# Mixing begun at the first half of the first value chunk, and the value pairs' weight sums formed on GpSimd

## The chip, the cores and the metric

The kernel runs on one core of one Trainium2 chip. A core has a matrix engine (TensorE, PE in the profile, whose weight loads are shown apart as PEld), three engines for elementwise work (VectorE or DVE, ScalarE or ACT, GpSimd or POOL) and SyncE (SP), which here only issues the transfers of weights. Each engine takes its instructions in the order in which they stand in its own queue and waits for the others through semaphores. The metric is the time of one execution in microseconds (us).

## The reference, cut to what matters

A trunk of two layers over 256 tokens and a model width of 2048, all in 32-bit floats. The change lies in the second layer, which is an mLSTM with 8 heads:

```python
hn = rmsnorm(h, o_norm[j])
u = hn @ o_w_in[j]                       # q|k (2048), v (2048), og (2048), z (2048), 16 gates
qk = jax.nn.silu(causal_conv(qk, c_conv_w[j], c_conv_b[j]))      # 4 taps
q, k = qk[..., :C_QK], qk[..., C_QK:]    # 8 heads of 128 each
li = ig + c_b_i[j]
lf = jax.nn.log_sigmoid(fg + c_b_f[j])
yc = mlstm(q, k, v.reshape(bsz, s, 8, 256), li, lf)
yc = head_rmsnorm(yc, c_norm[j]) * jax.nn.sigmoid(og) * jax.nn.silu(z)
h = h + yc @ o_w_out[j]
...
# mlstm, for every head:
wts = jnp.exp(dmat - m_t[..., None])              # decay weights from the gates
sc  = jnp.einsum('bhtd,bhsd->bhts', qc, kc) * wts # scores
num = ... + jnp.einsum('bhts,bhse->bhte', sc, vc) # scores times values
den = ... + jnp.sum(sc, axis=-1)
hout = num / jnp.maximum(jnp.abs(den), jnp.exp(-m_t))[..., None]
```

## The kernel before, in words

**Products.** A 32-bit product is made of three matmuls in the fast format of PE: each operand is split into a high part (`hi`) and a remainder (`lo`), and hi·hi, hi·lo and lo·hi are added. Weights come as tiles of 128x1024 (512 KB). SP loads a tile into a ring `raw` of five buffers; ACT casts it to `whi` (L137, or L221 in `split_weights`), DVE subtracts to get `wlo` (L138, or L222), and PE runs 12 matmuls of 512 columns on it for each half of the tokens. `whi` and `wlo` have four buffers each, so DVE has to write one `wlo` of 128x1024 for each tile that PE uses.

**Pairs of chunks.** The columns of a weight matrix are done in pairs of chunks of 512 (`seven`, L288 to L382). For one quarter of the contraction seven products take the place of eight (Strassen's scheme); they need *sums of weight tiles*. The tiles X and Y lie in buffers `ch`. One sum is formed by an accumulating transfer that GpSimd issues (`add_loaded`, L314), others by a two-operand addition of 128x1024 (`add`, L310): X+Y after product 5, and X+Z when products 2 and 6 are both done. The rest of the contraction (letters a and b) is done plainly with tiles from the ring. The string `a5a6.2aA7b.4F.bb` gives the order of the steps; a point, and every plain piece, lets the other work in hand (`lanes`) go one step on. At "A" the first half of the tokens of the first chunk is handed out, at "F" the second half.

**The value stage.** `value_halves` runs two such pairs over the value columns: pair 0 gives the chunks j = 0 and 1, pair 1 the chunks 2 and 3. `values` turns each half (hf = 0, 1) of a chunk into a high part `vt` (ACT, L1394) and a remainder `vl` (DVE, L1395).

**Mixing.** `mix(j)` handles the heads 2j and 2j+1: PE spreads the running maximum over the partitions (`spread`, L431, out of a tile `s` that DVE makes at L426), DVE forms `wt` (L1305, L1306), ACT takes its exponential (L1310, L1311); ACT and DVE split q and k into `qhl` and `khl` (L1322, L1323); PE forms the scores (L1329, and L1330 for a block that needs one matmul only); DVE multiplies them by `wt` (L1331); ACT casts them to `sh` (L1334), DVE makes `sl` (L1335); then PE multiplies scores by values into `nu` (L1349), for mix(0) with the values of chunk 0. The values of q and k come from `features`: for each, ACT's L1214 and L1215, six instructions of DVE (L1218, the taps) a pair of heads, tanh on ACT (L1221) and a last product on DVE (L1222). Before that the q and k columns take a way through memory, by transfers that GpSimd issues (L686, L689). `gate_stats` (L1257 to L1285) makes the maximum from the gate columns, in small instructions of DVE.

In the kernel before, the four mixes are started when the *second* half of chunk 0 has been handed out ("F" of pair 0). The program is written in that order, and a scheduler puts each instruction into its engine's queue by priorities that follow the order of the program, with splits, additions and mix's splits moved forward (`tc.high_priority`). So the place at which a lane is started decides where its matmuls stand among PE's products, and everything on the engines is in order behind it.

Of the kernel before, what the change touches and what calls it, by code (L numbers as in the profile page):

```python
# [16 lines left out]
ALU = mybir.AluOpType  # L17
# [28 lines left out]
def trunk(ctx: ExitStack, tc: tile.TileContext, a, out):  # L46
    nc = tc.nc
    v, s, gp, te, sy = nc.vector, nc.scalar, nc.gpsimd, nc.tensor, nc.sync
# [28 lines left out]
    def pump():  # L77
        with ExitStack() as behind:
            for ins in last.values():
                behind.enter_context(tc.issue_after(ins))  # L80
            for lane in list(lanes):
                step(lane)
# [40 lines left out]
    def block(src, c, n):  # L123
        return src[c * P:(c + n) * P].rearrange("(p n) -> p n", p=P)
# [92 lines left out]
    def split_weights(r):  # L217

        hi, lo = (wp.tile([P, 1024], F32R, name=n, tag=n) for n in ("whi", "wlo"))
        with tc.high_priority(offset=400):  # L220
            last["act"] = s.copy(hi, r).ins  # L221
            last["dve"] = v.tensor_tensor(out=lo, in0=r, in1=hi.bitcast(F32), op=ALU.subtract).ins  # L222
        return hi, lo
# [14 lines left out]
    def stationary(act, js, hf):  # L238
        return [[tokens(act[j][x], k, hf) for j in js for k in range(2)] for x in range(2)]

    def plain(w, j, kq, act, ps, first=(False, False), end=False):

        parts = load_weights(w[4 * j + kq])
        for hf in range(2):
            product(ps[hf], stationary(act, (2 * kq, 2 * kq + 1), hf), parts, first[hf], end)
            if hf == 0:
                pump()
# [37 lines left out]
        keep(d, (2, 4))  # L285
        yield

    def seven(w, j, act, qs, kqs, room, part, home=None, order=None, acc=None, before=None, third=None):  # L288

        def src(b, side, kq):  # L290
            return block(w[4 * (j + b) + kq], side * 1024, 1024)

        def load(tile_of, b, side):
            tiles = []
            for kq in kqs:
                t = tile_of()
                last["sp"] = sy.dma_start(out=t, in_=src(b, side, kq)).ins
                tiles.append(t)
            return tiles

        def ring():
            return wp.tile([P, 1024], F32, name="raw", tag="raw", bufs=5)

        def split(tiles):
            return [split_weights(t) for t in tiles]

        def add(x, y):
            with tc.high_priority(offset=400):
                for xi, yi in zip(x, y):
                    v.tensor_tensor(out=xi, in0=xi, in1=yi, op=ALU.add)  # L310

        def add_loaded(x):
            for xi, kq in zip(x, kqs):
                gp.dma_start(out=xi, in_=src(1, 0, kq), accum_op=ALU.add)  # L314

        def soon(out, in0, in1, op):
            with tc.high_priority(offset=450):
                v.tensor_tensor(out=out, in0=in0, in1=in1, op=op)

        def keep(out, bank):  # L320
            with tc.high_priority(offset=450):
                s.copy(out, bank)

        def quadrant(side, hf):
            return stationary(act, [2 * kq + side for kq in kqs], hf)

        def combo(n):
            return [[t for kq in kqs for t in qs[n, kq][x]] for x in range(2)]

        if acc is None:  # L330
            acc = len(kqs) == 2
        rest = [kq for kq in range(4) if kq not in kqs]
        E = px.tile([P, 512], F32, name="mx", tag="mx")
        A, F, B = (pm.tile([P, 512], F32, name="mm", tag="mm") for _ in range(3))
        b5, g = part(), part()
        rows = [list(rest), list(rest)]
        X = load(room, 0, 0)
        product(A, quadrant(0, 0), split(X), True)
        if acc:
            add_loaded(X)  # L340
        with tc.high_priority(offset=450):
            if home is not None:
                with tc.issue_after(last["act"]):
                    s.copy(E, home)
            s.copy(F, A)
            s.activation(B, F, AF.Copy, scale=-1.0)
        if third is not None:
            plain(w, j + 2, kqs[0], act, third, (True, True))
        Y = load(room, 1, 1)
        product(E, combo(4), split(Y), home is None)  # L350
        W = X
        if not acc:
            W = load(ring, 1, 0)
            add(Y, W)
            add(W, X)
        did = set()
        for op in order or ORDERS[len(kqs)]:
            if op in "ab":
                b = "ab".index(op)
                kq = rows[b].pop(0)  # L360
                if before is not None:
                    before(kq)
                plain(w, j + b, kq, act, ((A, F), (E, B))[b], end=not rows[b])
            elif op == "5":
                product(B, combo(1), split(W))
                add(X, Y)
                if acc:
                    add_loaded(Y)
                keep(b5, B)
            elif op == "6":  # L370
                product(B, combo(2), split(X))
                keep(g, B)
            elif op == "2":
                Z = load(ring, 0, 1)
                product(A, quadrant(1, 0), split(Z))
            elif op == "4":
                product(F, quadrant(1, 1), split(X))
            elif op == "7":
                product(B, combo(3), split(Y))
                soon(b5, B, b5, ALU.subtract)  # L380
            elif op == ".":
                pump()  # L382
            elif op == "A":
                yield 0, 0, A
            elif op == "F":
                soon(b5, F, b5, ALU.subtract)
                yield 0, 1, b5
            did.add(op)
            if op in "26" and {"2", "6"} <= did:
                add(X, Z)  # L390
        if home is None:
            soon(g, E, g, ALU.add)
            yield 1, 0, g
        else:
            soon(home, E, g, ALU.add)
            yield 1, 0, None
        yield 1, 1, B
# [243 lines left out]
    acth = []  # L641
# [133 lines left out]
    if True:  # L775
        ew = a["ew"]
        fs, qs, ks, xcs = {}, {}, {}, {}
# [281 lines left out]
        vts = []  # L1059
# [74 lines left out]
    act = out_proj(hq, mixed(), "fe")  # L1134
# [23 lines left out]
    acth = ple_gate(hq, two_and_seven(a["g0"], act, ready(act, "fe"), (e0, "q4", 2), in_e0), pls, rp0, hss0, "on", "fg", gate_sums)  # L1158
# [34 lines left out]
    with tc.tile_pool(name="m1", bufs=2) as m1:  # L1193
# [32 lines left out]
        qs = {}  # L1226
# [17 lines left out]
        vts = []  # L1244
# [132 lines left out]
        def value_halves():  # L1377
            drain("combos")
            pr = pieces(m1.tile([P, 1024], F32, name="pr", tag="vt", bufs=6))
            yield from seven(a["ov"], 0, acth, qs, (0,), chain, pr, acc=True)  # L1380
            drain("spill")
            store_of.extend(hp.tile([P, 1024], F32, name="pr", tag="h") for _ in range(2))
            for b, hf, src in seven(a["ov"], 2, acth, qs, (0,), chain, part, acc=True):
                yield 2 + b, hf, src

        def values():
            for j, hf, src in value_halves():
                if hf == 0:
                    vt = m1.tile([P, 2, 2, VW], F32R, name="vt", tag="vt", bufs=6)
                    gp.memset(vt.bitcast(F32)[:, :, :, 256:VW], 1.0)  # L1390
                    vl = ap.tile([P, 1024], F32R, name="vl", tag="ahl").rearrange("p (h i e) -> p h i e", h=2, i=2)
                with tc.high_priority(offset=450):
                    src = src.rearrange("p (i e) -> p i e", i=2)
                    s.activation(vt[:, hf, :, 0:256], src, AF.Copy, scale=norm["rt"][:, hf:hf + 1])  # L1394
                    v.scalar_tensor_tensor(vl[:, hf], src, norm["rt"][:, hf:hf + 1], vt[:, hf, :, 0:256].bitcast(F32),  # L1395
                                           op0=ALU.mult, op1=ALU.subtract)
                if hf == 0:
                    continue
                vts.append((vt, vl))
                if j == 0:  # L1400
                    drain("qk0", "qk2")
                    for c in range(4):
                        start("mix", mix(c))
                    start("mix", mix_norm())
# [4 lines left out]
        def part():  # L1409
            n = len(turn) % 4  # L1410
            turn.append(n)
            return store_of[n // 2][:, n % 2 * 512:(n % 2 + 1) * 512]
# [28 lines left out]
        for jj in (0, 2):  # L1441
            us = [m1.tile([P, 2, 512], F32, name="u", tag="vt", bufs=6) for _ in range(2)]
            for b, hf, src in pair(a["oz"], jj, True):
                j, u = jj + b, us[b]
# [59 lines left out]
        act, qs1 = {}, {}  # L1504
# [232 lines left out]
```

## Time and profile before

| | us |
|---|---|
| median of 3 runs | 1028.01 |
| lowest, highest | 1027.76, 1029.28 |
| the profiled execution | 1028.51 |
| its span | 1026.7 |

The profiled execution took 0.5 us more than the median, and 1.8 us of it lie outside of the span. The mean granted clock of PE was 0.994 of full speed. Times inside the trace are counted from the span's start. The value stage is the stretch from 561 us (first product of pair 0) to 649 us; pair 1 begins at about 605 us.

How such rows are read: in the page's list of engines, each engine has its busy time, its share of the span and its count of instructions. A row of the list of waits says which instruction waited for which, with the total, the times and the longest. A row of the timeline is: start, duration, engine, line, operation, output <- inputs, size, and in brackets the idle time just before it with what ended it. Durations of a row overlap with the next by the pipeline's depth, so the time that an instruction takes of its engine is read from start to start.

### The profile page before, as it was taken

The page shows a single profiled execution, that of the slowest core. Times are in us where ns is not written, and L with a number is a line of the kernel's source. Part 1 is how long each engine was busy: PE and PEld are TensorE (multiplying, and loading weights), DVE is VectorE, ACT ScalarE, POOL GpSimd, SP SyncE. Part 2 cuts the span into 40 slices and gives each one's busy share as a digit, 9 for nine tenths or more (in the row PEclk, how much of TensorE's full clock was granted, in tenths as well). Part 3 has the DMA queues.
Part 4 walks back from the last instruction along what each step waited for, and adds up shares of the span by engine and source line. Part 5 has one row for each costly group of instructions (what it writes and reads, how often), then busy time and mean ns, then how long its engine had stood idle before and what let it go on. Part 6 is the DMA issues. An engine that isn't in the chain of part 4 may idle for free.

```text
span 1026.7 us, 14530 instructions
## 1 busy us (share of the span) xinstructions
PE 1011.9 (99%) x5152; PEld 838.6 (82%) x5152; DVE 850.5 (83%) x1242; ACT 665.8 (65%) x956; POOL 103.5 (10%) x184
## 2 busy tenths in 40 slices
PE   9999999999999999999999999899999999999996
PEld 8888888888888888878888877688888888888886
DVE  7858968969686888879579998778989997899794
ACT  7775554686974555567557877676666867465562
POOL 0111101011111111022021100000011110111000
PEclk9999999999999999999999999899999999999998
DMA  9987756567688799588897856447879889686852
GB/s 360 335 223 250 222 175 203 167 200 238 221 263 303 246 298 286 165 263 254 290 314 217 263 166 219 163 155 204 251 194 296 237 236 354 198 284 210 283 184 83
DMA packets 69960, 243.18 MB, mean 237 GB/s; under 512 B 9056, under 2 KB 10464, under 8 KB 69888
## 3 DMA queue, kind: packets, MB, share of 16 engines
q1 hardware_dynamic: 55872, 197.56, 57.5%
q0 software_dynamic: 13584, 44.18, 16.4%
q8 instruction: 40, 0.66, 0.3%
q10 hardware_dynamic: 432, 0.52, 0.1%
q14 instruction: 32, 0.26, 0.1%
HBM read 222.31 MB, written 19.92 MB: 236 GB/s over the span
## 4 chain that ended last, share of the span: by engine, by line
PE 89%; DVE 7%; issue 1%; ACT 1%; DMA 1%; ACTq 0%; DVEq 0%; POOLq 0%
PE mm L235 27%; PE mm L211 12%; PE mm L213 12%; PE mm L212 12%; PE mx L235 8%; PE mx L213 3%; PE mx L212 3%; PE mx L211 3%; DVE wlo L138 2%; DVE qk L1218 2%; DVE wlo L222 1%; PE mm L517 1%; PE nu L1349 1%; PE mx L517 1%; PE mm L1562 1%
## 5 line engine op out<-in xcount | busy, mean ns | idle before, releaser
L138 DVE TENSOR_TENSOR wlo<-raw,whi 128x1024 fp32r<-128x1024 f32 (+1 forms) x305 | 366.1, 1211 | 101.8 <-ACT whi L137 96.2
L137 ACT CAST whi<-raw 128x1024 fp32r<-128x1024 f32 (+1 forms) x305 | 318.0, 1046 | 202.5 <-PE mm L213 84.4
L235 PE MATMUL mm<-whi,ahl 128*128 128x512 f32 x804 | 258.4, 390 | 0.0
L211 PE MATMUL mm<-whi,ahl 128*128 128x512 f32 x576 | 225.3, 392 | 0.0
L212 PE MATMUL mm<-wlo,ahl 128*128 128x512 f32 x576 | 224.2, 389 | 0.0
L213 PE MATMUL mm<-whi,ahl 128*128 128x512 f32 x576 | 224.1, 389 | 0.0
L235 PEld LDWEIGHTS mm<-whi,ahl 128*128 128x128 f32 x804 | 150.7, 188 | 31.1
L235 PE MATMUL mm<-wlo,ahl 128*128 128x512 f32 x402 | 156.7, 390 | 0.0
L211 PEld LDWEIGHTS mm<-whi,ahl 128*128 128x128 f32 x576 | 108.1, 188 | 23.0 <-issue 0.4
L213 PEld LDWEIGHTS mm<-whi,ahl 128*128 128x128 f32 x576 | 108.1, 188 | 22.5
L212 PEld LDWEIGHTS mm<-wlo,ahl 128*128 128x128 f32 x576 | 108.2, 188 | 22.0
L222 DVE TENSOR_TENSOR wlo<-ch,whi 128x1024 fp32r<-128x1024 f32 x73 | 88.2, 1219 | 11.3 <-ACT whi L221 9.6
L221 ACT CAST whi<-ch 128x1024 fp32r<-128x1024 f32 x73 | 76.2, 1049 | 26.4 <-PE mm L235 13.9
L235 PEld LDWEIGHTS mm<-wlo,ahl 128*128 128x128 f32 x402 | 75.5, 188 | 15.5
L235 PE MATMUL mx<-whi,ahl 128*128 128x512 f32 x216 | 71.3, 390 | 0.0
L235 PE MATMUL mm<-whi,q 128*128 128x512 f32 x156 | 53.1, 390 | 0.0
L211 PE MATMUL mx<-whi,ahl 128*128 128x512 f32 x128 | 49.8, 389 | 0.0
L212 PE MATMUL mx<-wlo,ahl 128*128 128x512 f32 x128 | 49.8, 389 | 0.0
L213 PE MATMUL mx<-whi,ahl 128*128 128x512 f32 x128 | 49.8, 389 | 0.0
L235 PEld LDWEIGHTS mx<-whi,ahl 128*128 128x128 f32 x216 | 40.5, 188 | 8.7 <-issue 0.4
L235 PE MATMUL mx<-wlo,ahl 128*128 128x512 f32 x108 | 42.2, 391 | 0.0
L235 PEld LDWEIGHTS mm<-whi,q 128*128 128x128 f32 x156 | 29.3, 188 | 6.2
(389 smaller groups left out, 1344.7 us busy)
## 6 DMA issues: line engine op xcount, KB each, us to landing
raw<-in_ew_dram SPq DMA_DIRECT2D x64, 512.0 KB, 4.9
raw<-in_g_dram SPq DMA_DIRECT2D x60, 512.0 KB, 4.6
raw<-in_oqk_dram SPq DMA_DIRECT2D x32, 512.0 KB, 5.2
raw<-in_eo_dram SPq DMA_DIRECT2D x30, 512.0 KB, 4.9
raw<-in_oo_dram SPq DMA_DIRECT2D x30, 512.0 KB, 6.6
raw<-in_ov_dram SPq DMA_DIRECT2D x26, 512.0 KB, 4.6
raw<-in_oog_dram SPq DMA_DIRECT2D x24, 512.0 KB, 4.5
raw<-in_oz_dram SPq DMA_DIRECT2D x20, 512.0 KB, 4.5
```

What stands on the lines that cost most here:

```text
L137: last["act"] = s.copy(h, r).ins
L138: last["dve"] = v.tensor_tensor(out=l, in0=r, in1=h.bitcast(F32), op=ALU.subtract).ins
L211: te.matmul(ps[hf], xh, wh, start=(k == 0), stop=False, skip_group_check=True)
L212: te.matmul(ps[hf], xh, wl, start=False, stop=False, skip_group_check=True)
L213: last["pe"] = te.matmul(ps[hf], xl, wh, start=False, stop=(k == KT - 1), skip_group_check=True).ins
L221: last["act"] = s.copy(hi, r).ins
L222: last["dve"] = v.tensor_tensor(out=lo, in0=r, in1=hi.bitcast(F32), op=ALU.subtract).ins
L235: last["pe"] = te.matmul(o, x, y, start=(first and k + i == 0), stop=(end and k == n - 1 and i == 2), skip_group_check=True).ins
L517: last["pe"] = te.matmul(ps[hf][:, o:o + w_], tokens(pact[x], k, hf), (hi, lo)[y][:, k * 512 + o:k * 512 + o + w_], start=(n == mine[0]), ...
L1218: v.scalar_tensor_tensor(dst[:, sh:T], pi[:, 0:T - sh], pc("ccw", k * 16 + n), dst[:, sh:T], op0=ALU.mult, op1=ALU.add)
L1349: te.matmul(ps[:, 0:n], x[:, i, o:o + P], y[:, b, i], start=(b == 0 and x is sh and y is vh), stop=(b == hf and y is vl))
L1562: te.matmul(o, xh, wl, start=False, stop=False)
```

## The change

Two edits. `seven` gets an argument `adds`, the engine that forms the sums of weight tiles in `add`: VectorE as before for all callers but the two value pairs, which pass GpSimd. And `values` starts the four mixes when the *first* half of chunk 0 has been handed out ("A" of pair 0 instead of "F"), in the turn ahead of the one in which `vts` gets the chunk; `mix(j)` still waits for its values by the test of `vts`. From L1397 on, lines of the changed kernel are one lower than before.

```diff
-    def seven(w, j, act, qs, kqs, room, part, home=None, order=None, acc=None, before=None, third=None):
+    def seven(w, j, act, qs, kqs, room, part, home=None, order=None, acc=None, before=None, third=None, adds=v):
...
                 for xi, yi in zip(x, y):
-                    v.tensor_tensor(out=xi, in0=xi, in1=yi, op=ALU.add)
+                    adds.tensor_tensor(out=xi, in0=xi, in1=yi, op=ALU.add)
...
-            yield from seven(a["ov"], 0, acth, qs, (0,), chain, pr, acc=True)
+            yield from seven(a["ov"], 0, acth, qs, (0,), chain, pr, acc=True, adds=gp)
...
-            for b, hf, src in seven(a["ov"], 2, acth, qs, (0,), chain, part, acc=True):
+            for b, hf, src in seven(a["ov"], 2, acth, qs, (0,), chain, part, acc=True, adds=gp):
...
-                if hf == 0:
-                    continue
-                vts.append((vt, vl))
-                if j == 0:
+                if hf:
+                    vts.append((vt, vl))
+                elif j == 0:
                     drain("qk0", "qk2")
                     for c in range(4):
                         start("mix", mix(c))
```

What this does to the engines' queues is not in the diff. First PE, at the scores of mix(0). Before, they stand in pair 1, one or two at a time between matmuls of the products (L235), 82 of which lie between the end of pair 1's first product and the first of the scores:

```order
L235 MATMUL mm<-whi,ahl 128x512 x2
L1329 MATMUL mx<-qhl,khl 128x256 x2
L235 MATMUL mm<-wlo,ahl 128x512
L235 MATMUL mm<-whi,ahl 128x512 x2
L235 MATMUL mm<-wlo,ahl 128x512
L1329 MATMUL mx<-qhl,khl 128x256
L1330 MATMUL mx<-qk 128x128
L235 MATMUL mm<-whi,ahl 128x512 x2
L235 MATMUL mm<-wlo,ahl 128x512
L1329 MATMUL mx<-qhl,khl 128x256 x3
L1330 MATMUL mx<-qk 128x128
L235 MATMUL mm<-whi,ahl 128x512 x2
```

Now, PE again, directly behind pair 1's first product (its last five matmuls are shown):

```order
L235 MATMUL mm<-whi,ahl 128x512 x2
L235 MATMUL mm<-wlo,ahl 128x512
L235 MATMUL mm<-whi,ahl 128x512
L1329 MATMUL mx<-qhl,khl 128x256 x4
L1330 MATMUL mx<-qk 128x128
L1329 MATMUL mx<-qhl,khl 128x256 x2
L1330 MATMUL mx<-qk 128x128
L1349 MATMUL nu<-vt,sh 128x258 x4
L431 MATMUL mx<-s_5488,identr 128x256 x2
L1349 MATMUL nu<-vt,sl 128x258
L1349 MATMUL nu<-vl,sh 128x256
```

Scores, scores times values and the spread for mix(1) have moved ahead of 82 matmuls, and stand together: 12 more rows of L1349 follow, and only then the next product. Nothing that PE could do meanwhile stands between the rows that depend on each other.

Second DVE, at the same mix(0). Before, the three rows of `khl` (for mix(0), mix(1) and mix(2), in this order) lie among splits of weights:

```order
L138 TENSOR_TENSOR wlo<-raw,whi 128x1024
L1323 TENSOR_TENSOR khl<-qk,khl 128x256
L1222 SCALAR_TENSOR_TENSOR qk<-th,qk 128x512
L1306 TENSOR_TENSOR wt<-cst,mx 128x2x128
L1323 TENSOR_TENSOR khl<-qk,khl 128x256
L1331 SCALAR_TENSOR_TENSOR wt<-mx,wt 128x384 x2
L138 TENSOR_TENSOR wlo<-raw,whi 128x1024
L1323 TENSOR_TENSOR khl<-qk,khl 128x256
L1335 TENSOR_TENSOR sl<-wt,sh 128x768
```

Now, DVE:

```order
L138 TENSOR_TENSOR wlo<-raw,whi 128x1024
L1218 SCALAR_TENSOR_TENSOR qk<-xr,prm,qk 128x253
L222 TENSOR_TENSOR wlo<-ch,whi 128x1024
L1218 SCALAR_TENSOR_TENSOR qk<-xr,prm,qk 128x254
L1218 SCALAR_TENSOR_TENSOR qk<-xr,prm,qk 128x253
L1222 SCALAR_TENSOR_TENSOR qk<-th,qk 128x512
L1323 TENSOR_TENSOR khl<-qk,khl 128x256 x2
L1331 SCALAR_TENSOR_TENSOR wt<-mx,wt 128x384 x2
L1335 TENSOR_TENSOR sl<-wt,sh 128x768
```

The two rows of `khl` are those of mix(0) and mix(1); mix(0)'s stands directly behind an L1222 of another head's k, and on ACT its high part (L1322) stands behind the tanh (L1221) that this L1222 reads. From L1257 (an early instruction of `gate_stats`) to the `khl` row of mix(0), this one included, DVE had 91 instructions and has 79 now: four additions (L310), eight splits of weights (five L138, three L222) and two L1395 stand no longer ahead of it, one L1222 and one L1306 are new ahead of it. No split of weights stands any more between `khl` and `sl`.

Third GpSimd, in pair 0 and at the start of pair 1, as it is now (before, the rows L310 were not there, and the four L689 stood together):

```order
L314 DMA ch<-in_ov_dram 128x1024
L686 DMA dqk_5331<-w 128x1024
L310 ISA
L310 TENSOR_TENSOR ch<-ch 128x1024
L689 DMA r<-dqk_5331 32x4x256 x2
L310 TENSOR_TENSOR ch<-ch,raw 128x1024
L689 DMA r<-dqk_5331 32x4x256 x2
L314 DMA ch<-in_ov_dram 128x1024
L1390 MEMSET vt 128x4x2
L314 DMA ch<-in_ov_dram 128x1024
L310 TENSOR_TENSOR ch<-ch 128x1024
L314 DMA ch<-in_ov_dram 128x1024
```

The row marked ISA loads the code for the addition; it stands once, ahead of the first addition. The transfers that GpSimd issues (L689, which bring q or k back, and L314) now stand behind additions in its queue. The fourth addition follows the last row shown.

## The prediction

> **What bounds the kernel now.** I read the page first: who is busy,
>
> ```profile
> PE 1011.9 (99%) x5152; PEld 838.6 (82%) x5152; DVE 850.5 (83%) x1242; ACT 665.8 (65%) x956; POOL 103.5 (10%) x184
> ```
>
> and what the chain that ended last is made of.
>
> ```profile
> PE 89%; DVE 7%; issue 1%; ACT 1%; DMA 1%; ACTq 0%; DVEq 0%; POOLq 0%
> ```
>
> PE is busy 99% of the span, so the kernel can become faster only by what PE waits for, and any new wait of PE counts in full. The second view is therefore the list of PE's waits.
>
> ```profile
> PE nu L1349 <- ACT sh L1334: 4.4, 1, 4.4
> PE mx L431 <- DVE s L426: 0.8, 1, 0.8
> PE st L99 <- PEq L1728: 0.8, 1, 0.8
> PE mx L517 <- ACT whi L486: 0.3, 1, 0.3
> PE mx L1329 <- ACT khl L1322: 0.2, 1, 0.2
> PE mx L1329 <- DVE khl L1323: 0.2, 1, 0.2
> ```
>
> The first, second, fifth and sixth belong to the mixing lanes that the change moves. The third view is the timeline of PE, which gives their places.
>
> ```profile
> 603.71 0.50 PE L431 MATMUL mx<-s,identr 128*128 128x256 f32 x2 [0.81 <-DVE s L426]
> ...
> 625.58 0.50 PE L1329 MATMUL mx<-qhl,khl 128*128 128x256 f32 x2 [0.24 <-ACT khl L1322]
> ...
> 663.80 1.20 PE L1349 MATMUL nu<-vt,sh 128*128 128x258 f32 x4 [4.35 <-ACT sh L1334]
> ```
>
> A long wait costs more than itself. The windows view (columns: PE, PEld, DVE, ACT and POOL busy with counts, then PE's granted clock) shows that PE got half its clock behind the wait of 4.35 us:
>
> ```profile
> 666.00:667.00 1.00, 1.00 (x6) 1.00 (x6) 0.54 (x2) 1.00 (x3) 0.00 (x0) 0.50 0.04 16
> 668.00:669.00 1.00, 1.00 (x5) 0.90 (x4) 0.50 (x2) 0.90 (x4) 0.00 (x0) 0.54 0.00 0
> 669.00:670.00 1.00, 1.00 (x6) 0.78 (x6) 1.00 (x5) 0.88 (x3) 0.00 (x0) 1.00 0.00 0
> ```
>
> From 663.80 to about 668.97 PE worked 5.17 us at half clock, which would have been 2.58 us at full clock: 2.58 us lost. All that mixing costs PE before is so 0.81 + 0.24 + 0.2 + 4.35 + 2.58 = **8.2 us**, and this is the most that the change can win.
>
> The last view is DVE's groups in the stretch from 564.5 to 627.2 us, in which it works off what stands ahead of mix(0) (count, busy time, mean ns, idle time before them).
>
> ```profile
> L138 DVE TENSOR_TENSOR wlo<-raw,whi 128x1024 fp32r<-128x1024 f32 x17 | 20.5, 1214 | 0.7 <-ACT whi L137 0.6
> L222 DVE TENSOR_TENSOR wlo<-ch,whi 128x1024 fp32r<-128x1024 f32 x9 | 10.9, 1216 | 0.2
> L1218 DVE SCALAR_TENSOR_TENSOR qk<-xr,prm,qk 128x255 f32<-128x255 f32 (+2 forms) x24 | 10.6, 473 | 0.0
> ```
>
> Its costliest group waits 0.7 us in 62, the next ones 0.2 and nothing: DVE is full there, and what it has to do before `khl` sets when `khl` comes.
>
> **The change part by part: DVE's queue.** The queue from L1257 to mix(0)'s `khl` begins and ends at these rows, 62.2 us apart:
>
> ```profile
> 564.54 0.27 DVE L1257 MEMSET ae<- 64x256 f32 x1
> ...
> 566.16 1.23 DVE L310 TENSOR_TENSOR ch<-ch 128x1024 f32<-128x1024 f32 x1
> 567.30 1.22 DVE L138 TENSOR_TENSOR wlo<-raw,whi 128x1024 fp32r<-128x1024 f32 x1
> ...
> 583.18 0.75 DVE L1395 SCALAR_TENSOR_TENSOR vl<-mm,rcr,vt 128x512 fp32r<-128x512 f32 x1
> 583.85 0.33 DVE L1269 TENSOR_SCALAR xf<-xf,prm 8x256 f32<-8x256 f32 x1
> ...
> 626.75 0.42 DVE L1323 TENSOR_TENSOR khl<-qk,khl 128x256 fp32r<-128x256 f32 x1
> 627.08 0.69 DVE L1222 SCALAR_TENSOR_TENSOR qk<-th,qk 128x512 f32<-128x512 f32 x1
> 627.68 0.42 DVE L1306 TENSOR_TENSOR wt<-cst,mx 128x256 f32<-128x256 f32 x1
> ```
>
> From start to start an operation of 128x1024 takes 1.14 us (566.16 to 567.30), an L1395 0.67, an L1222 0.60, an L1306 about 0.3. The order rows say what is different ahead of `khl`: four additions and eight splits fewer, 12 x 1.14 = 13.6; two L1395 fewer, 1.3; one L1222 and one L1306 more, 0.9. That is 14.0 us less, so DVE could start `khl` at 626.75 - 14.0 = 612.7. One wait is new: the last taps of DVE, the tanh on ACT and L1222 now follow one another without other work between, and ACT's high part of `khl` stands behind this tanh.
>
> ```profile
> 624.60 0.64 ACT L1221 ACTIVATE th<-qk 128x512 f32<-128x512 f32 x1 [0.27 <-DVE qk L1218]
> 625.14 0.39 ACT L1322 CAST khl<-qk 128x256 fp32r<-128x256 f32 x1
> ```
>
> I take the tanh's row and a tenth, 0.75 us. So `khl` starts at 613.5 and is whole at 613.9.
>
> **PE's demand moves further than DVE's supply.** The scores move ahead of 82 matmuls of 512 columns; twelve of these take 2.72 us on the chain:
>
> ```profile
> 670.14 2.72 PE mm L235 x12
> ```
>
> 82 x 0.2267 = 18.6. PE reached them at 625.58 - 0.24, and without the 0.81 of L431 (whose place moves too, 44 matmuls ahead) it gets there at 625.34 - 18.6 - 0.8 = 605.9. **This is the point of the case: PE comes 19.4 us earlier, `khl` only about 13.** Three of the scores' matmuls may start with the high part; the fourth needs the low part at 613.9. PE loses about 613.9 - 605.9 - 0.2 = 7.8 us. If PE is late earlier, at a product whose split DVE delivers late, part of it shows there; the end is the same.
>
> Behind the scores nothing covers PE either: L1331, the cast `sh`, then `nu`.
>
> ```profile
> 628.64 1.19 DVE L1331 SCALAR_TENSOR_TENSOR wt<-mx,wt 128x384 f32<-128x384 f32 x2
> ```
> ```profile
> 630.70 0.84 ACT L1334 CAST sh<-wt 128x768 fp32r<-128x768 f32 x1
> ```
>
> Half of the 1.19 (one head's product after its scores) and the cast make 1.4 us, some 0.2 between engines: 1.6. `sl`, of fewer columns than a split of weights, lies beside four `nu` and the two of L431, about 1.2 us at half clock. A wait of several us brings the half clock again: its size is that of the row of before, 2.6. For mix(1) to mix(3) I count 1.1 us: DVE, with 14 us less, has room, but the values of chunk 1 become ready as PE comes for them. Sum of what is new: 7.8 + 1.6 + 2.6 + 1.1 = 13.1; what goes, if the later mixes are in time: 8.2. **Net +4.9 us.**
>
> **The additions on GpSimd.** No row before shows one. The nearest on this engine writes 128x512 in 0.52 us, and its waits and transfers are these:
>
> ```profile
> L1141 POOL MEMSET wg<- 128x512 f32 x1 | 0.5, 520 | 12.6 <-ACT ahl L151 12.6
> ```
> ```profile
> 564.83 0.57 POOL L686 DMA_DIRECT2D dqk<-w  x1 [5.89 <-DVE ae L1257]
> 567.94 0.87 POOL L314 DMA_DIRECT2D ch<-in_ov_dram  x1 [2.54 <-DVE ch L310]
> 570.81 2.23 POOL L689 DMA_DIRECT2D r<-dqk  x4 [2.00 <-DMA dqk<-w]
> ```
>
> 1024 columns by that row are 1.04 us if only the output counts, 3.1 if each of two inputs costs as much; I take 2.1 (two of three). Three additions lie ahead of or beside the critical stretch: two in pair 0, and pair 1's first. What they cost is how far DVE is held beside them. From below this is nothing, as different engines; a gain below nothing is left out, since the gain of a shorter DVE queue is in the sum already. From above it is their whole length, 3 x 2.1 = 6.3, or 3 x 3.1 = 9.3 with the longest. I take about half, 1.1 each, **+3.3 us**; it is also what the same operation takes of DVE. On POOL, two L689 come behind the second addition, some 2 to 3 us later; their readers are taps in the queue of DVE well ahead of its limit, so nothing is counted. The load of code stands behind L686, from about 565.4 on. ACT reads the first sum at 573 in my walk through its new queue, so 5.5 us of loading are covered by ACT's other work (573 - 565.4 - 2.1); beyond that each us costs one. The nearest row is a table load on ACT:
>
> ```profile
> 589.89 1.28 ACT L1273 ACT_TABLE_LOAD   x1
> ```
>
> With 1.28 it is hidden, and counts nothing; twice the covered length would cost 5.5.
>
> The Trainium skill, SBUF — State Buffer, section "Who interferes with whom", speaks against the change: a VectorE instruction with two inputs in SBUF and a GpSimd instruction that reads SBUF take one shared port, and whoever comes second stands still for the whole instruction. Nearly all of DVE's rows here (L138, L222, L1222, L1323) are of that kind; by it the hold is the rival of a full hold below, which no run shows so far. The GPSIMD Engine Reference of the Trainium skill, section 3.1, has 4497 ns for an addition of 2048 columns, by which one here would take, as an estimate, 2.2 us; its section 2.1 has about 6 us for the first call after a load, by which 0.5 us would be left uncovered.
>
> **The sum.** On the profiled execution: 1028.51 + 4.9 + 3.3 = 1036.7. That execution is 0.5 us above the median, so 1036.2 against 1028.01.
>
> **The rivals.**
>
> *DVE held for the whole of every addition.* For it: DVE's operations there have two inputs like the additions; against it: no row of before has the two beside each other. 1028.0 + 4.9 + 6.3 = 1039.2, with the longest additions 1042.2.
>
> *DVE not held.* 1028.0 + 4.9 = 1032.9. For it: L314 and L689 of POOL lie beside DVE's 128x1024 operations at 1.14 us each with no lengthening (567.94 beside 567.30); but these are issues of transfers, not arithmetic.
>
> *A load of code that isn't covered.* Each us above 5.5 adds one; at twice that, 1036.2 + 5.5 = 1041.7.
>
> *Even.* The new waits are as large as those that go: `khl` by 609.3 instead of 613.9 (a loss of 3.2 there, 8.5 in all), if ACT and DVE run taps of k ahead of what I took. Then about 1028.
>
> *Faster, the other side.* If `khl` is there when PE comes, at 606, and `sh` in its wake, the waits of mix(0) and the one of 4.35 us go with their half clock, and 8.2 us are won: 1019.8. The point from which it decides is 8 us of DVE's queue: the 24 taps (L1218, 10.6 us) and the tanh would have to be done beside the last products of layer work ahead of 564 us. Against it: 626.75 - 564.54 - 14.0 = 48.2 us of DVE's work lie between, with next to no wait that could be filled.
>
> That the change doesn't do what it says I leave out: the order rows show the additions on POOL and the scores moved.
>
> **How the numbers follow.** Forecast 0.36, full hold 0.24, no hold 0.15, uncovered load 0.05, even 0.10, faster 0.10. The first four are slower by over 0.2% (2.06 us, about what a measurement here can tell from no change): 0.80; within: 0.10; faster: 0.10. The range leaves out the last two: from 1029.5 (no hold, and 3 us less at the scores) to 1042.5 (full hold with the longest additions).
>
> **What would show it.** Right: PE's list has waits of 5 to 8 us in all at L1329 for `khl` between 605 and 614, and one of 1.5 to 2 at `nu` for `sh`; half clock behind them; no 4.35 near 663; L138 and L222 that lie beside an L310 of POOL last well over 1.22 us (a hold), between 1.2 and 2.2. Wrong: no wait at L1329 (the faster case); L138 beside L310 at 1.22 (no hold); a gap on POOL of over 5.5 us ahead of its first L310, with ACT waiting for it (the load); or a wait of PE at a place that no sentence here names, such as an accumulated tile that comes late behind an addition.

## The result and the profile after

| | us |
|---|---|
| before, median (1027.76 to 1029.28) | 1028.30 |
| changed, median of 4 runs (1042.32 to 1045.91) | 1042.68 |
| ratio, 95% interval | 1.0146 (1.0124 to 1.0167) |
| the changed kernel's profiled execution, its span | 1042.57, 1040.8 |

The change makes the kernel 1.46% slower, some 14.4 us. The forecast was slower, by 8.2 us, with a range up to 1042.5: the direction is right, the size is not, and the time lies just above the range.

The page of the changed kernel, engines and chain: PE is busy a little longer and for a smaller share of a longer span, and the chain now lies on PE to 94%.

```profile
PE 1015.4 (98%) x5152; PEld 840.5 (81%) x5152; DVE 855.0 (82%) x1238; ACT 666.3 (64%) x956; POOL 113.8 (11%) x188
...
PE 94%; DVE 2%; ACT 1%; DMA 1%; issue 1%; POOL 0%; ACTq 0%; POOLq 0%
```

DVE has four additions fewer (1242 - 4 = 1238 instructions) and yet is busy 855.0 us in place of 850.5. That is the first hint: a lengthened instruction counts as busy.

PE's list of waits of the changed kernel:

```profile
PE mx L1329 <- ACT khl L1322: 7.0, 1, 7.0
PE mm L235 <- ACT whi L221: 4.9, 1, 4.9
PE nu L1349 <- ACT sh L1334: 1.6, 1, 1.6
PE mm L235 <- DVE wlo L138: 1.5, 1, 1.5
...
PE mx L431 <- ACT sq L1355: 0.5, 1, 0.5
```

The waits of 0.8 at L431 and of 4.35 at mix(2) are gone. The first and the third row are the ones that were forecast, though the first wait ends at 623 us, some ten us later than forecast. The second, 4.9 us at a product of pair 0, was not. Its place is in PE's timeline:

```profile
591.90 0.79 PE L235 MATMUL mm<-whi,q 128*128 128x512 f32 x1 [4.91 <-ACT whi L221]
593.16 0.79 PE L235 MATMUL mm<-wlo,q 128*128 128x512 f32 x1 [0.47 <-DVE wlo L222]
...
623.20 1.35 PE L1329 MATMUL mx<-qhl,khl 128*128 128x256 f32 x4 [6.96 <-ACT khl L1322]
```

This is product 7, which reads the split of Y after Y got its accumulating transfer. The timeline of GpSimd tells why that split is late:

```profile
565.89 2.38 POOL L310 TENSOR_TENSOR ch<-ch 128x1024 f32<-128x1024 f32 x1 [0.72 <-DVE wlo L222]
...
577.02 3.31 POOL L310 TENSOR_TENSOR ch<-ch,raw 128x1024 f32<-128x1024 f32 x1 [5.13 <-DVE wlo L222]
580.28 1.09 POOL L689 DMA_DIRECT2D r<-dqk  x2
581.36 0.98 POOL L314 DMA_DIRECT2D ch<-in_ov_dram  x1
```

Y's transfer (L314) is issued at 581.36; before it was issued at 567.94, as soon as X+Y was done on VectorE, and ahead of the four L689 of 570.81 (the prediction shows both rows). Now it stands in GpSimd's queue behind X+Z, which waits for a split until 577.02 and takes 3.3 us. What was said of this queue ahead of the prediction leaves the move out: it names the new additions and the parted L689 only. The program still writes Y's transfer ahead of X+Z (`add_loaded` at step 5 of the order), but `add` has the high priority and `add_loaded` has none. In ACT's timeline the landing follows 9.4 us after the issue (5.7 and 7.5 for the two such transfers of pair 0 before), and only then can the cast begin:

```profile
590.80 1.04 ACT L221 CAST whi<-ch 128x1024 fp32r<-128x1024 f32 x1 [2.58 <-DMA ch<-in_ov_dram]
```

And DVE's timeline beside the additions at 565.89, 577.02 and 619.41:

```profile
566.03 3.33 DVE L138 TENSOR_TENSOR wlo<-raw,whi 128x1024 fp32r<-128x1024 f32 x1 [0.22 <-ACT whi L137]
...
578.00 4.56 DVE L138 TENSOR_TENSOR wlo<-raw,whi 128x1024 fp32r<-128x1024 f32 x2
...
619.24 2.95 DVE L1218 SCALAR_TENSOR_TENSOR qk<-xr,prm,qk 128x254 f32<-128x254 f32 x2
```

A split takes 1.22 elsewhere, two 2.35, two taps 0.87. Each of the three groups is 2.1 to 2.2 us longer. (The fourth addition, at 641.52, lies behind the scores; a split beside it takes 3.01.) The first split ends its stay on DVE 1.0 us after the addition (569.28 against 568.27), as if it had begun only then. The second addition shows the opposite: it begins while a split of DVE runs (until 578.00) and takes 3.31 in place of 2.38.

Where the time went, in PE's terms: in pair 0 the waits are 0.3 + 1.5 + 4.9 + 0.5 = 7.2, and the clock is at half from 591.90 to about 598.2, some 5.8 us of work, which loses 2.9. The windows view of the changed kernel (the clock is the third number from the end):

```profile
597.00:598.00 1.00, 1.00 (x3) 0.73 (x3) 1.00 (x2) 0.97 (x4) 0.00 (x0) 0.50 0.80 279
598.00:599.00 1.00, 1.00 (x6) 0.80 (x5) 0.97 (x2) 1.00 (x3) 0.00 (x0) 0.95 0.88 315
629.00:630.00 1.00, 1.00 (x7) 1.00 (x6) 0.89 (x2) 0.47 (x2) 0.00 (x0) 0.50 0.00 0
632.00:633.00 1.00, 1.00 (x6) 0.80 (x5) 0.40 (x5) 0.89 (x3) 0.00 (x0) 0.89 0.00 0
```

At the scores: 7.0 + 1.6, half clock from 623.20 to about 632.2 (7.4 us without the wait of 1.6), which loses 3.7; later 0.5. Together 7.2 + 2.9 + 7.0 + 1.6 + 3.7 + 0.5 = 22.9, against the 8.2 that are gone: 14.7, and the profiled executions differ by 1042.57 - 1028.51 = 14.1.

### The profile page after: what moved, and what is told of

Its sections match the earlier page's. It is cut to its first block, busy times and chain, and to the rows that moved or that the text cites. A ratio compares the mean times of both kernels' runs of the same rounds, so it can differ in the third digit from the quotient of the medians.

```text
span 1040.8 us, 14517 instructions
## 1 busy us (share of the span) xinstructions
PE 1015.4 (98%) x5152; PEld 840.5 (81%) x5152; DVE 855.0 (82%) x1238; ACT 666.3 (64%) x956; POOL 113.8 (11%) x188
## 4 chain that ended last, share of the span: by engine, by line
PE 94%; DVE 2%; ACT 1%; DMA 1%; issue 1%; POOL 0%; ACTq 0%; POOLq 0%
PE mm L235 29%; PE mm L211 13%; PE mm L212 13%; PE mm L213 13%; PE mx L235 9%; PE mx L213 3%; PE mx L212 3%; PE mx L211 3%; PE mm L517 1%; DMA ch<-in_ov_dram 1%; PE nu L1349 1%; PE mx L517 1%; DVE qk L1218 1%; PE mm L1561 1%; PE mm L1562 1%
## 5 line engine op out<-in xcount | busy, mean ns | idle before, releaser
L138 DVE TENSOR_TENSOR wlo<-raw,whi 128x1024 fp32r<-128x1024 f32 (+1 forms) x305 | 370.6, 1226 | 106.4 <-ACT whi L137 100.6
L235 PE MATMUL mm<-whi,ahl 128*128 128x512 f32 x804 | 258.4, 390 | 0.0
L235 PEld LDWEIGHTS mm<-whi,ahl 128*128 128x128 f32 x804 | 150.9, 188 | 31.4
L235 PE MATMUL mm<-wlo,ahl 128*128 128x512 f32 x402 | 156.6, 390 | 1.5 <-DVE wlo L138 1.5
L222 DVE TENSOR_TENSOR wlo<-ch,whi 128x1024 fp32r<-128x1024 f32 x73 | 88.4, 1220 | 13.7 <-ACT whi L221 12.2
L235 PEld LDWEIGHTS mm<-wlo,ahl 128*128 128x128 f32 x402 | 75.5, 188 | 17.4 <-DVE wlo L138 1.9
L235 PE MATMUL mx<-whi,ahl 128*128 128x512 f32 x216 | 72.2, 395 | 0.0
L235 PE MATMUL mm<-whi,q 128*128 128x512 f32 x156 | 54.4, 397 | 4.9 <-ACT whi L221 4.9
L235 PEld LDWEIGHTS mx<-whi,ahl 128*128 128x128 f32 x216 | 41.2, 191 | 9.0 <-ACT whi L137 0.4
L235 PE MATMUL mx<-wlo,ahl 128*128 128x512 f32 x108 | 42.6, 394 | 0.0
L235 PEld LDWEIGHTS mm<-whi,q 128*128 128x128 f32 x156 | 29.8, 191 | 11.5 <-ACT whi L221 5.3
```

The costliest lines, as they stand in the source:

```text
L138: last["dve"] = v.tensor_tensor(out=l, in0=r, in1=h.bitcast(F32), op=ALU.subtract).ins
L235: last["pe"] = te.matmul(o, x, y, start=(first and k + i == 0), stop=(end and k == n - 1 and i == 2), skip_group_check=True).ins
```

## The experiments

My theory after this reading has three causes: the scores ahead of DVE's supply, DVE held by GpSimd's additions, and Y's transfer behind X+Z. The rivals are that one of them does it all.

**1. The additions alone** (the changed kernel with the old start of the mixes):

```diff
-                if hf:
-                    vts.append((vt, vl))
-                elif j == 0:
+                if hf == 0:
+                    continue
+                vts.append((vt, vl))
+                if j == 0:
```

> Only the additions go to GpSimd; the mixes start at the old place. My theory (three causes: an accumulating transfer late behind an addition in GpSimd's queue; DVE held about 2.1 us beside each addition; PE's scores moved ahead of DVE's supply): the first two stay, so PE's wait of 4 to 6 us for a sum near 590 us is here too, L138 of 3.3 us beside an addition too, and the time is 1031 to 1036. Rival, the early mixing alone is the cause: no such wait, 1027 to 1029.

1033.44 us, ratio 1.0043 (1.0026 to 1.0059). PE's list has the wait of product 7 again, and L138 lasts 3.33 us beside the first addition.

```profile
PE mm L235 <- ACT whi L221: 4.9, 1, 4.9
```

So the late transfer comes with the additions. The 4.35 of mix(2) is not there either: with the additions elsewhere the scheduler puts mix(0)'s scores 50 matmuls earlier (596 of L235 ahead of them, 646 before).

**2. The early mixing alone** (the kernel before with the second edit; the additions stay on VectorE):

```diff
-                if hf == 0:
-                    continue
-                vts.append((vt, vl))
-                if j == 0:
+                if hf:
+                    vts.append((vt, vl))
+                elif j == 0:
```

> Only the early start of the mixes; the additions stay on VectorE. My theory: no wait near 590 us, PE waits 8 to 11 us at the scores (L1329) and 1.6 us at nu, because DVE still has the three additions (3.4 us) in place of the holds (6.3 us): 1034 to 1037. Rival, GpSimd's additions alone are the cause: the scores are in time and the time is 1026 to 1029.

1034.97 us, ratio 1.0062 (1.0047 to 1.0077). From PE's list and its timeline:

```profile
PE mx L1329 <- ACT khl L1322: 9.6, 1, 9.6
PE nu L1349 <- issue: 1.6, 1, 1.6
```
```profile
615.96 1.35 PE L1329 MATMUL mx<-qhl,khl 128*128 128x256 f32 x4 [9.55 <-ACT khl L1322]
```

This edit costs some 6 us by itself. Its new waits lie at the place that the prediction named, but for one at L517 that grew from 0.3 to 1.0, and PE comes there at 615.96 - 9.55 = 606.4.

**3. The transfer first** (the changed kernel, with Y's transfer given the priority of the additions; it then stands ahead of X+Z in GpSimd's queue):

```diff
         def add_loaded(x):
-            for xi, kq in zip(x, kqs):
-                gp.dma_start(out=xi, in_=src(1, 0, kq), accum_op=ALU.add)
+            with tc.high_priority(offset=400 if adds is gp else 0):
+                for xi, kq in zip(x, kqs):
+                    gp.dma_start(out=xi, in_=src(1, 0, kq), accum_op=ALU.add)
```

> The changed kernel, with one thing more: the accumulating transfers of the value pairs get the priority of the additions, so that Y's stands in GpSimd's queue directly behind X+Y and ahead of X+Z, as it did before the change. My theory: PE's wait of 4.9 us near 590 us and the half clock behind it are gone, PE then waits longer at the scores since DVE's holds remain: 1037 to 1040. Rival, DVE's holds alone set the end: the wait moves to the scores entirely, 1041.5 to 1043.

1039.15 us, ratio 1.0103 (1.0088 to 1.0118). The transfer is issued at 571.65, the wait of 4.9 is gone, and the one at the scores grows to 10.4 (line numbers are one higher here):

```profile
571.65 0.94 POOL L315 DMA_DIRECT2D ch<-in_ov_dram  x1
```
```profile
PE mx L1330 <- ACT khl L1323: 10.4, 1, 10.4
```

By the medians the late transfer is worth 1042.68 - 1039.15 = 3.5 us on top of the rest: less than its own 8 us of wait and clock, since a PE that is later waits less at the scores.

**4. The sums by transfers** (as experiment 3, but the sums formed by accumulating transfers from buffer to buffer, so that GpSimd computes nothing):

```diff
-                    adds.tensor_tensor(out=xi, in0=xi, in1=yi, op=ALU.add)
+                    if adds is gp:
+                        gp.dma_start(out=xi, in_=yi, accum_op=ALU.add)
+                    else:
+                        v.tensor_tensor(out=xi, in0=xi, in1=yi, op=ALU.add)
```

> As the run before (transfers first, early mixing), but the sums X+Y and X+Z of the value pairs are formed by accumulating transfers from buffer to buffer instead of GpSimd's arithmetic, so that no instruction of GpSimd reads beside DVE. My theory of DVE held 2.1 us by each addition: L138 stays at 1.2 us throughout, the scores come some 4 to 6 us earlier than in the run before, 1031 to 1036, unless the transfers' own 5 us delay a split. Rival, GpSimd's additions don't hold DVE in a way that matters: no better than the run before, 1037 to 1043.

1038.67 us, ratio 1.0093 (1.0078 to 1.0108): the time lies in the range of the rival (no better than experiment 3), though the holds are gone. DVE's timeline (L222 and L138 as before) has no lengthened split, this one included (1.23), but a new wait:

```profile
576.03 1.23 DVE L222 TENSOR_TENSOR wlo<-ch,whi 128x1024 fp32r<-128x1024 f32 x1 [4.34 <-ACT whi L221]
```

The sum arrives by transfer after its way through the queue, ACT waits for it, and DVE behind ACT waits 4.3 us. A new loss came with the end of the holds, so this run neither shows the price of the holds nor that they have none.

**5. Kinds of work on GpSimd** (the kernel before, with work on a scratch tile of 128x256 that nothing reads):

```diff
+                    scr = m1.tile([P, 256], F32, name="scr", tag="scr", bufs=1)
+                    gp.memset(scr, 0.0)
+                for _ in range(6):
+                    if (j, hf) in ((0, 0), (2, 0)):
+                        gp.tensor_tensor(out=scr, in0=scr, in1=scr, op=ALU.add)
+                    elif (j, hf) in ((0, 1), (2, 1)):
+                        gp.memset(scr, 0.0)
+                        gp.memset(scr, 0.0)
+                    elif (j, hf) in ((1, 0), (3, 0)):
+                        gp.tensor_copy(scr, scr)
+                    else:
+                        gp.tensor_scalar(scr, scr, 1.0, None, op0=ALU.add)
```

> The kernel before, with work on GpSimd that nothing reads, on a tile of 128x256: additions of two inputs, fills that read nothing, copies and additions of a constant with one input each, six to twelve in a row, beside VectorE's splits and taps (two inputs each). My theory, VectorE with two inputs can't run beside a GpSimd instruction that reads the same memory: VectorE's operations beside the additions and the copies are lengthened by up to one GpSimd instruction each, those beside the fills stay at 1.22 us (128x1024) and 0.47 us (taps). Rival, GpSimd being busy at all slows VectorE: lengthened beside the fills too. Other rival, only two-input GpSimd work does it: lengthened beside additions alone.

This kernel ran once, and its time (1039.68) isn't compared. It shows a late transfer a second time, with the additions on VectorE and the old start: X's accumulating transfer stands behind the scratch work in GpSimd's queue and is issued at 566.45 (558.01 before), ACT's cast waits for it, and PE waits 7.2 us for what stands behind this cast.

```profile
573.68 1.04 ACT L221 CAST whi<-ch 128x1024 fp32r<-128x1024 f32 x1 [8.71 <-DMA ch<-in_ov_dram]
```

GpSimd's timeline has copies and constants (537.94 to 549.3), additions (549.78 to 555.7) and fills (561.52 to 564.8):

```profile
537.94 4.96 POOL L1401 COPY scr<-scr 128x256 f32<-128x256 f32 x6
...
549.78 1.65 POOL L1396 TENSOR_TENSOR scr<-scr 128x256 f32<-128x256 f32 x2
...
563.75 0.31 POOL L1399 MEMSET scr<- 128x256 f32 x1
```

DVE's timeline beside them:

```profile
539.08 1.41 DVE L138 TENSOR_TENSOR wlo<-raw,whi 128x1024 fp32r<-128x1024 f32 x1
...
549.33 4.35 DVE L1218 SCALAR_TENSOR_TENSOR qk<-xr,prm,qk 128x255 f32<-128x255 f32 x6
553.61 3.19 DVE L138 TENSOR_TENSOR wlo<-raw,whi 128x1024 fp32r<-128x1024 f32 x2
...
557.32 2.45 DVE L1218 SCALAR_TENSOR_TENSOR qk<-xr,prm,qk 128x255 f32<-128x255 f32 x6
...
563.23 2.32 DVE L138 TENSOR_TENSOR wlo<-raw,whi 128x1024 fp32r<-128x1024 f32 x2
```

Beside the additions six taps take 4.35 in place of 2.45, two splits 3.19 in place of 2.32: 2.8 us for six additions, some 0.5 for each, and an addition by itself takes 0.61 here (509.33). Beside the fills nothing changes (2.32). Beside the copies a split takes 1.41 in place of 1.22, a lengthening of 0.2, well under the 0.53 that a copy takes by itself (four in 2.14 at 567.07). So GpSimd's being busy is not enough to hold DVE, and the first rival falls: the fills write and don't read. Of the second rival a part is left: work with one input does lengthen DVE's operations, but much less than the additions do.

**6. The scores later** (experiment 2, with two more turns in mix(0) before q and k are split, so that 655 in place of 564 matmuls of L235 stand ahead of the scores; before the change they were 646):

```diff
             if j == 0:
-                yield
+                for _ in range(3):
+                    yield
```

> Early start of the mixes with the additions on VectorE, as in the run of the early mixing alone, but mix(0) lets two more turns pass before it makes q and k ready, which puts its scores 91 matmuls of the products later in PE's queue. My theory, the early start costs only through the place of the scores ahead of VectorE's supply: the waits of 9.6 and 1.6 us and the half clock go, 1021 to 1029. Rival, the early start costs by buffers and banks held longer, wherever the scores stand: 1032 to 1036.

1027.76 us, ratio 0.9995 (0.9985 to 1.0004). With the early start kept, the wait at the scores is 0.8 in place of 9.6, and the time is that of before: what the early start costs, it costs by where it puts the scores, and the rival (buffers and banks held longer) falls. A wait of 3.8 us at 664 us is there, as one was before.

**7. The kernel before, score steps first:**

```diff
-                v.scalar_tensor_tensor(wt[:, i, :], sc[:, 0:384], SC, wt[:, i, :], op0=ALU.mult, op1=ALU.mult)
+                with tc.high_priority(offset=450):
+                    v.scalar_tensor_tensor(wt[:, i, :], sc[:, 0:384], SC, wt[:, i, :], op0=ALU.mult, op1=ALU.mult)
...
-            s.copy(sh, wt)
-            v.tensor_tensor(out=sl, in0=wt, in1=sh.bitcast(F32), op=ALU.subtract)
+            with tc.high_priority(offset=450):
+                s.copy(sh, wt)
+                v.tensor_tensor(out=sl, in0=wt, in1=sh.bitcast(F32), op=ALU.subtract)
```

> The kernel before, with one thing changed: the products of scores and weights (L1331) and the split of their result (L1334, L1335) get the priority that q's and k's splits have. My theory, the 4.35 us wait of mix(2) before stood only on L1331 behind two additions and three splits in VectorE's queue: that wait and its half clock go (6.9 us), 1021 to 1025, if PE's scores don't move ahead of supply again. Rival, something else is late next (the values, psum banks): 1026 to 1030.

1027.05 us, ratio 0.9988 (0.9979 to 0.9997): the rival (something else is late next) holds. The wait of 4.35 went, and this one came, for a psum bank that ACT's square of `nu` frees; the square itself waits for a copy (L1355 here, `den`) that stands in DVE's queue behind three additions and three splits:

```profile
665.21 0.79 PE L235 MATMUL mx<-whi,q 128*128 128x512 f32 x1 [3.64 <-ACT sq L1357]
```
```profile
664.68 0.38 ACT L1357 ACTIVATE sq<-nu 128x256 f32<-128x256 f32 x1 [0.87 <-DVE den L1355]
```

**8. The additions on GpSimd, old start, transfer first** (experiment 1 with the edit of experiment 3):

> The additions on GpSimd and the mixes started at the old place, and the accumulating transfers of the value pairs with the priority of the additions, so that Y's is issued ahead of X+Z. My theory, most of what the additions alone cost (1033.4 against 1028.9) is the late transfer with its wait of 4.9 us and half clock; VectorE's holds are covered where mix(0) comes late: 1026 to 1030. Rival, the holds cost it without the early mixing too: 1031 to 1034.

1030.01 us, ratio 1.0019 (1.0010 to 1.0029), just above the 1026 to 1030 that I expected and under the rival's 1031. Without the early mixing the late transfer is worth 1033.44 - 1030.01 = 3.4 us, and the rest of the additions on GpSimd 1.7 us more than VectorE's. This 1.7 is a balance and not the price of the holds: as in experiment 1, the wait of 4.35 with its half clock (6.9 us) is gone, and in its place PE waits for splits of DVE, as in these rows (line numbers are one higher):

```profile
579.45 0.50 PE L235 MATMUL mm<-wlo,q 128*128 128x512 f32 x1 [1.32 <-DVE wlo L222]
583.94 0.50 PE L235 MATMUL mm<-wlo,ahl 128*128 128x512 f32 x1 [1.48 <-DVE wlo L138]
628.21 0.38 PE L1330 MATMUL mx<-qhl,khl 128*128 128x256 f32 x1 [1.90 <-DVE qhl L1324]
```

**9. The kernel before, all of mixing's steps first** (experiment 7, with the reads of `nu` too):

```diff
-                    s.copy(o, ps[:, 0:256])
-                    v.tensor_copy(den[:, c:c + 1], ps[:, 256:257])
                     sq = tp.tile([P, 512], F32, name="sq", tag="sq", bufs=1)[:, 0:256]
-                    s.activation(sq, ps[:, 0:256], AF.Square, accum_out=ss[:, c:c + 1])
+                    with tc.high_priority(offset=450):
+                        s.copy(o, ps[:, 0:256])
+                        v.tensor_copy(den[:, c:c + 1], ps[:, 256:257])
+                        s.activation(sq, ps[:, 0:256], AF.Square, accum_out=ss[:, c:c + 1])
```

> As the run of the kernel before with the score steps ahead (L1331, L1334, L1335 with priority), and the reads of the result (L1352, L1353, L1355) with the same priority, since there the wait moved to a psum bank that ACT's square frees after a copy that stands late in VectorE's queue. My theory, that was what was late next: the 3.6 us and its half clock go, 1019 to 1024. Rival, a fourth wait takes its place: 1025 to 1028.

1022.32 us, ratio 0.9946 (0.9929 to 0.9962): 5.5 us (by the ratio) faster than the kernel before and 20 faster (by the medians) than the changed one, with the additions on VectorE and the old start. The long wait is gone; the two longest of PE are now

```profile
PE mx L517 <- ACT whi L486: 1.1, 1, 1.1
PE mx L431 <- DVE s L426: 0.8, 1, 0.8
```

## Why the prediction was right in direction and wrong in size

- **"PE comes 19.4 us earlier, `khl` only about 13": right as a mechanism.** Experiment 2 has PE there at 606.4 (605.9 forecast) and a wait of 9.6 us with the additions still on DVE; experiment 6 takes the wait away by moving the scores later. In the changed kernel both ends come some ten us later than forecast: PE at 623.20 - 6.96 = 616.2, since it had lost 10.1 in pair 0, and DVE's `khl` at 623.50 in place of 613.5, since DVE had been held for 6.3 and had waited for late work, 1.7 of it for Y's cast. That 7.0 is left of the forecast 7.8 is therefore partly luck; without the late transfer (experiment 3) it is 10.4.
- **The steps behind the scores: right in kind.** The wait for `sh` is 1.6, as forecast. The half clock was mis-sized: 3.7 us against 2.6, since the wait of 1.6 lies inside it and 7.4 us of work follow the first wait. Later mixes cost 0.5 against 1.1.
- **"All that mixing costs PE before" goes: right** for the 4.35 and the 0.8. With 12.8 at the scores in place of 13.1 this part of the sum came out, with the luck that was just named.
- **The hold of DVE: mis-sized.** I took "about half, 1.1 each"; the trace has 2.1 to 2.2 for each of three additions, 6.3 in place of 3.3. The rival of a full hold, at 0.24, was the true case for the holds: experiment 3, which has them but not the late transfer, took 1039.15, and the rival's sum was 1039.2. The rule of the Trainium skill, SBUF — State Buffer, "Who interferes with whom", that VectorE with two inputs and a GpSimd instruction that reads exclude each other for a whole instruction, agrees with the rows of 566.03 and 577.02, in both directions. The copies of experiment 5, which lengthened a split by 0.2 only, don't show a stop for a whole instruction. What I gave for it, that nothing of before had the two beside each other, was no reason for a half.
- **The step that failed: GpSimd's queue.** I wrote that "two L689 come behind the second addition" and that "nothing is counted". For the L689 that holds: no wait of PE names their readers. But I looked only at them: Y's L314 stands behind the same addition in the order rows, where before it stood ahead of all four L689, and its reader is product 7. The last of the prediction's signs of being wrong, "an accumulated tile that comes late behind an addition", names just this, but it had no price in the sum. It costs 3.5 us (experiment 3 against the changed kernel, by medians), 3.4 without the early mixing (experiment 8 against 1). Counted from the kernel before as it was measured beside each of these runs (1028.30, 1028.86, 1028.29), the two are 4.1 and 2.9, so they are good to some 0.6 us.
- **The load of code: right that it is hidden.** L686 ends at about 565.2 and the first addition starts at 565.89, after 0.72 us, released by a split of DVE; no gap of several us shows.

The sum as it should have been: 1036.2 + 3.0 for the holds + 3.5 for the transfer = 1042.7, against 1042.68 measured. The 3.5 is itself a difference of measured times, so what agrees here is only 1036.2 + 3.0 = 1039.2 with the 1039.15 of experiment 3. That is partly luck, since the terms aren't independent: the two edits alone cost 4.4 and 6.4 us by their ratios, 10.8 together, and both at once 15.0. The traces show one reason for this excess of 4.2. The wait of 4.35 with its half clock, 6.9 us together, is gone in the kernels with one edit (experiments 1, 2 and 8) as in the kernel with both. It can be won only once, so the two edits taken alone count it twice. How the rest of the terms act on each other is not shown. With the early mixing, the additions on GpSimd without the late transfer cost 1039.15 - 1034.97 = 4.2 us (experiment 3 against 2), without it 1.7 (experiment 8), a balance in which that gain stands.

What stays open is the price of the holds apart from all else: the one run without them (experiment 4) brought a late sum in their place.

## What to carry to other kernels

Moving work to an idle engine pays only if the engine that is relieved isn't held by it: here each of three additions took 1.14 us off VectorE's queue and stopped it for 2.1. When instructions with high priority are put on an engine that also issues transfers, read the whole of its queue for what now stands behind them, and follow each of these to its reader. And before a consumer is moved earlier, compare how far it moves with how far its supply moves; here the consumer moved 19 us and the supply about 10 (the scores of experiment 2 began at 615.96, those of before at 625.58), and the better cure for the old wait (experiment 9) was to move the short steps of mixing ahead in the queues of DVE and ACT.

## What the runs showed of the hardware

- GpSimd's addition of 128x1024 takes 2.38 us by itself, twice VectorE's 1.22. VectorE and GpSimd stop each other when both work on two inputs: a split of 1.22 took 3.33 beside an addition, and an addition that met a split took 3.31. They don't simply take turns: in experiments 1 and 8 the first addition of pair 1 met several operations of VectorE in a row and took 4.65 and 4.30. Fills on GpSimd (128x256, 0.31 us each) stopped nothing; copies with one input lengthened a split by 0.2 us.
- Half clock after a wait of PE: from the wait's end it lasted 6.3 us behind the wait of 4.9 (591.90 to 598.2), and 9.0 us behind the wait of 7.0 with one of 1.6 in it.
